# Attention on one core: VectorE's share of the exponentials without a mask pass, nine groups in place of eight, the last head's products in a score buffer

## The chip, the core and the metric

The kernel runs on one core of a Trainium2 chip. A core has a matrix engine (TensorE, "PE" in the profile; its weight loads are "PEld"), a vector engine (VectorE, "DVE"), an activation engine (ScalarE, "ACT"), a general engine (GpSimd, "POOL") and a queue engine (SyncE, "SP") that here only issues transfers. They share an on-chip memory (SBUF) with 128 partitions and an accumulator memory (PSUM) that TensorE writes. The metric is the device time of one execution in microseconds (us); lower is better.

## What is computed

Softmax attention for 8 x 8 heads, each with 512 queries, 512 keys and a width of 64, in float32:

```
scores = einsum('bhqd,bhkd->bhqk', q, k) / sqrt(64)
attn   = exp(scores - rowmax);  attn = attn / rowsum
out    = einsum('bhqk,bhkd->bhqd', attn, v)
```

That is 64 heads x 512 x 512 = 16.8 million exponentials. The kernel leaves the row maximum out (the ratio is the same without it), works with fp16 operands, and gets the row sum from a column of ones that stands beside the values.

## The kernel before, in words

**Tiling.** Two heads make a pair, 32 pairs in all. The scores of one head are computed transposed, in four blocks of 128 keys x 512 queries. Two blocks make a group: one PSUM tile `st` of 128 x 1024 float32, of which there are three. There are 129 groups (the last two hold one block each); the first three are written out by hand in `first_pair`.

**The road of a group.** GpSimd casts q and k of a pair to fp16 (`cast`, L335; the values in L329). TensorE transposes them (`transposes`, L388), VectorE copies the transposes to SBUF (`copy`, L402), TensorE makes the two score blocks (`scores`, L425), and the exponential turns `st` into fp16 weights `pt`. Of the groups, most go to ScalarE (one activation, L430). The eight listed in `ON_DVE` go to VectorE: `raise_` (L447) scales the scores out of PSUM into a fixed-point integer `z`, whose high half will be the bits of an fp16 number; the first `pass_` (L463) masks the fraction out of `z` into `m`; four more passes (L475) evaluate a polynomial in `m` and add it to `z`, and the result's high half, read as fp16, is the exponential. All six work on 128 x 1024 elements; the raise reads PSUM, the other five read and write SBUF.

**Products.** For each 128 queries of a head, four matmuls with the weights as the stationary operand add up 128 x 65 outputs (`values`, L514): a unit. Seven units share a PSUM bank tile `o`, of which there are two, shared with the transposes. VectorE takes a reciprocal and multiplies (`normalise`, L489 and L491), and SP writes the head out (L500). The last head is done block by block as its exponentials come (`last_values`, L529), into one of these two tiles; its 128 x 256 results go out through two queues (L549).

**Order.** All engines work through fixed lists. Class `Plan` makes the order: it steps through time with a cost for each kind of work (`SLOT`, `EXP`, `COPY`, `NORM`, `RAISE`, `PASSES`, `V_UNIT`), gives TensorE scores when one of the three `st` is free and otherwise transposes or products, and gives VectorE a pass of the exponential only where no copy, norm or raise would become late by it (`LATE_COPY`, `LATE_NORM`; a pass's cost is multiplied with `MARGIN`). Loads are issued by SP six pairs ahead (`feed`). GpSimd's casts are held back (`hold`, `release`) and given a wait on a VectorE instruction, so that they begin at a raise, copy or norm.

**Start.** ScalarE and SP load k and q of the first pair head by head. `make_identity` builds the identity on GpSimd. Four casts of the first head follow, one of them on GpSimd (k of two tiles, L579, then q of the second head, L581). TensorE runs eight matmuls without use (L562), transposes (L600, L595), and waits in order: the second transpose of k needs GpSimd's cast, and the first scores (L605) stand behind it.

Of the kernel before, what the change touches and what calls it, by code (L numbers as in the profile page):

```python
# [7 lines left out]

FP32 = mybir.dt.float32
FP16 = mybir.dt.float16  # L10
U32 = mybir.dt.uint32

EXP = mybir.ActivationFunctionType.Exp
# [3 lines left out]
class Plan:  # L17
# [18 lines left out]
    COPY, NORM, RAISE = (615, 700), (307, 390), (1145, 1225)  # L36
    COPY_1 = (400, 490)
    NORM_COLUMN, PASS_DONE = 67, 80
    PASSES = (650, 1230, 1230, 1230, 1230)
    FIRST_EXP = 5260  # L40
    STEP = 5
    FIRST_UNIT = 4
    ON_DVE = (6, 19, 30, 45, 62, 78, 90, 101)

    LATE_NORM, LATE_COPY, HURRY, SOON, BACKLOG = 1300, 1400, 900, 80, 1000
    MARGIN, SLACK = 1.05, 0

    def __init__(self, groups, pairs, first):
        self.groups, self.pairs = groups, pairs
        self.pe, self.act, self.dve = 7000, self.FIRST_EXP, 7000  # L50
        self.m, self.tiled = first, True
        self.read = []
        self.exps = {}
        for m in range(first):
            self.act += self.EXP + self.EXP_FIXED
            self.exps[m] = self.act + self.EXP_DONE
            self.read.append(self.exps[m])
        self.tq = {0: 5800}
        self.next_t = 1
        self.part_t = 0  # L60
        self.banks = [5100, 5800]
        self.todo = [(g, h) for g in range(pairs) for h in range(2)]
        self.head = None
        self.units = self.FIRST_UNIT
        self.member = {b: m for m, grp in enumerate(groups) for b in grp}
        self.ready = []
        self.passes = []
        self.steps = []
# [20 lines left out]
    def scores(self, t):  # L89
        m, grp = self.m, self.groups[self.m]  # L90
        slots = 2 if len(grp) == 2 and 0 < grp[0][0] and grp[0][2] == grp[1][2] else 1
        on_dve = self.for_dve(m)
        if m % 4 == 0 and grp[0][0] > 0 and len(grp) == 2:
            self.note(t, "feed", grp[0][0])
        self.note(t, "scores", m, on_dve)
        t += (0 if self.tiled else self.INTO) + self.SLOT * slots
        self.tiled = True
        if on_dve:
            self.ready.append((t + self.TO_DVE, "raise", (m,)))
            self.read.append(1e9)  # L100
        else:
            begin = max(self.act, t + self.TO_ACT)
            self.act = begin + self.EXP * len(grp) // 2 + self.EXP_FIXED
            self.exps[m] = self.act + self.EXP_DONE
            self.read.append(self.exps[m])
        self.m += 1
        self.pe = t
# [19 lines left out]
            self.part_t = 0  # L127

    def wants(self, g, h, part):

        chunks = (part,) if (g, h) == (self.pairs - 1, 1) else range(4)
        return max(self.exps.get(self.member[(g, c, h)], 1e9) for c in chunks)

    def edge(self):

        u, first = self.units, self.FIRST_UNIT
        return u % 7 == 0 or u in (first, first + 8 * self.pairs - 4)

    def values(self, t):
        if self.head is None:  # L140
            for g, h in self.todo[:14]:
                if t >= self.wants(g, h, 0) and t >= self.ready_v(g):
                    break
            else:
                return False
            if self.edge() and self.bank(t) is None:
                return False
            self.todo.remove((g, h))
            self.head = (g, h, 0)
# [10 lines left out]
        self.note(t, "values", g, h, part, self.units, self.bank_v)  # L160
        self.full(t, self.V_UNIT)
        self.units += 1
        if self.edge() and (g, h) != (self.pairs - 1, 1):
            what = (self.begun, self.units - self.begun, self.bank_v)
            self.ready.append((self.pe + self.TO_DVE, "norm", what))
        self.head = (g, h, part + 1) if part < 3 else None
# [54 lines left out]

    def run(self):
        t = 0
        while self.m < len(self.groups) or self.todo or self.head or self.ready or self.passes:
            if t >= self.pe:
                self.step_pe(t)
            if t >= self.dve:
# [8 lines left out]
def kernel(  # L236
# [45 lines left out]
    ring = cpool.tile([P, NU, D], FP32, name="ring")  # L282
    vps = [cpool.tile([P, 2, NI, D + 1], FP16, name=f"vp{n}") for n in range(NV)]
    ident = cpool.tile([P, P], FP16, name="ident")
    ones = nc.const_aps.tensor(1.0, [P, S], mybir.dt.bfloat16)

    raw = {}
# [119 lines left out]
    def scores(m, on_dve):  # L407
# [2 lines left out]
        st = ps_st.tile([P, 2, S], FP32, tag="st", name=f"st_{m}")  # L410
        if on_dve:
            bits = dpool.tile([P, 2, S], U32, tag="pd", name=f"pd_{m}")
            pt = bits.bitcast(FP16).rearrange("p x (s n) -> p x s n", n=2)[:, :, :, 1]
        else:
            pt = ppool.tile([P, 2, S], FP16, tag="pt", name=f"pt_{m}")
        for x, (g, c, h) in enumerate(grp):
# [4 lines left out]
            else:  # L421
                s = slice(64 * h, 64 * h + 64)
                kc = tqk[g][s, 1, c * P : (c + 1) * P]
                qc = tqk[g][s, 0, :]
            nc.tensor.matmul(st[:, x, :], kc, qc, start=True, stop=True)  # L425
            blocks[(g, c, h)] = pt[:, x, :]
        if on_dve:
            raised[m] = {"st": st, "bits": bits}
# [8 lines left out]

    QUARTIC = (0.013185735294320473 * 2.0**-78, 0.1618325836988675 * 2.0**-26, -0.6832878102805021, 0.5087543266551143 * 2.0**26)  # L440

    def raise_(m):
        release(2)
        r = raised[m]
        r["z"] = wpool.tile([P, 2, S], U32, tag="z", name=f"z_{m}")
        dve(
            nc.vector.tensor_scalar(  # L447
                out=r["z"][:, :, :],
                in0=r["st"][:, :, :],
                scalar1=scale * 1.4426950408889634 * 2.0**26,  # L450
                scalar2=15 * 2.0**26,
                op0=AluOp.mult,
                op1=AluOp.add,
            )
        )

    def pass_(m, s):
        r = raised[m]
        if s == 0:
            r["m"] = wpool.tile([P, 2, S], U32, tag="m", name=f"m_{m}")  # L460
            r["y"] = wpool.tile([P, 2, S], FP32, tag="y", name=f"y_{m}")
            dve(
                nc.vector.tensor_scalar(  # L463
                    out=r["m"][:, :, :],
                    in0=r["z"][:, :, :],
                    scalar1=0x03FFFFFF,
                    scalar2=0x04000000,
                    op0=AluOp.bitwise_and,
                    op1=AluOp.bitwise_or,
                )  # L470
            )
            return
        n = s - 1
        dve(
            nc.vector.scalar_tensor_tensor(  # L475
                out=r["bits"][:, :, :] if n == 3 else r["y"][:, :, :],
                in0=r["m"][:, :, :] if n == 0 else r["y"][:, :, :],
                scalar=QUARTIC[n],
                in1=r["z"][:, :, :] if n == 3 else r["m"][:, :, :],
                op0=AluOp.mult if n == 0 else AluOp.add,  # L480
                op1=AluOp.add if n == 3 else AluOp.mult,
            )
        )

# [18 lines left out]

    def values(g, h, y, u, bank):

        if (g, h) == (LAST, 1):
            return last_values(y, bank)
        if y == 0:
            needed(g, "v")
            heads.append((g, h, u))  # L510
# [8 lines left out]
                stop=(c == NI - 1),  # L519
            )  # L520

    def last_values(c, bank):


        if c == 0:
            last["o"] = ps_x.tile([P, 7, D + 1], FP32, tag=f"x{bank}", name="o_last")
        o = last["o"]
        for x in range(NI):
            nc.tensor.matmul(  # L529
# [123 lines left out]
    with tc.manual_schedule():  # L653
# [9 lines left out]
        for g in (1, 4, 5):  # L663
            load(g, "v")
        make_identity(nc, ident)
        for n in range(NV):
            nc.vector.memset(vps[n][:, :, :, D : D + 1], 1.0)
        first_pair()
        for g, names in ((1, "kq"), (0, "v"), (2, "kq")):
# [8 lines left out]
            "raise": raise_,  # L678
            "copy": lambda g, b: copy(g),
            "pass": pass_,  # L680
            "norm": lambda u, n, b: normalise(u, n),
        }
        for what, *args in Plan(groups, NP, 3).run():
# [31 lines left out]
```

## Time and profile before

| | |
|---|---|
| time, three runs | 121.89, 122.06, 122.09 us; median 122.06 |
| span of the profiled execution | 120.3 us; its time around the span is not listed, the median is 1.8 us more |
| ScalarE busy | 112.9 us (94% of the span) |
| VectorE busy | 105.1 us (87%) |
| TensorE busy, as modelled | 102.5 us (85%) |
| GpSimd busy | 64.5 us (54%) |
| HBM traffic | 25.17 MB read, 8.39 MB written; 279 GB/s over the span |
| granted TensorE clock | 0.998 of full speed over the span |

The profile is of one execution. A row for a group of instructions gives the engine, the operation, output and inputs, how many there were, their busy time and mean length, and the idle time of that engine just before them with what ended it. The length of a VectorE or ScalarE row includes its last stage, so the next row of the engine often begins a little before the row ends; how fast an engine goes through equal rows is read from the distance of their starts. TensorE's ends are modelled, and GpSimd's rows are rough.

### The profile page before, as it was taken

How to read it: one execution, taken by the hardware profiler on the slowest of the kernel's cores; microseconds unless marked ns; L12 is line 12 of the kernel's file. 1: busy time of each engine (PE TensorE's matmuls, PEld its weight loads, DVE VectorE, ACT ScalarE, POOL GpSimd, SP SyncE). 2: the span in 40 equal slices, each digit the busy share in tenths (PEclk: the TensorE clock that was granted, in tenths of full speed). 3: DMA queues.
4: the chain of work that ended last, by engine and by line, in shares of the span. 5: the costliest groups of instructions: out<-in, count | busy, mean ns of one | idle time of the engine just before them, and what ended most of it. 6: DMA issues, size and time to landing. Idle time of an engine off the chain costs nothing.

```text
span 120.3 us, 4002 instructions
## 1 busy us (share of the span) xinstructions
PE 102.5 (85%) x1557; PEld 64.7 (54%) x1557; DVE 105.1 (87%) x177; ACT 112.9 (94%) x125; POOL 64.5 (54%) x101
## 2 busy tenths in 40 slices
PE   7969478986999898988997999888899869999970
PEld 2536135644656564746664566644666536676650
DVE  1548999999999999999999999998999998996261
ACT  4699999999999999999999999999999999999970
POOL 2368867999649655359544557285546524340000
PEclk9999999999999999999999999999999999999999
DMA  3999999999999999899999898999999951232353
GB/s 102 293 346 379 381 380 385 383 377 332 312 361 355 339 352 346 277 303 306 284 299 296 228 376 256 300 362 349 325 304 357 301 187 44 90 120 95 106 166 96
DMA packets 35604, 33.83 MB, mean 281 GB/s; under 512 B 2688, under 2 KB 35584, under 8 KB 35584
## 3 DMA queue, kind: packets, MB, share of 16 engines
q1 hardware_dynamic: 35152, 33.24, 83.9%
q10 hardware_dynamic: 432, 0.33, 0.8%
q8 instruction: 12, 0.20, 0.7%
q14 instruction: 8, 0.07, 0.2%
HBM read 25.17 MB, written 8.39 MB: 279 GB/s over the span
## 4 chain that ended last, share of the span: by engine, by line
ACT 40%; PE 28%; DVE 22%; issue 8%; ACTq 0%
ACT pt L430 40%; PE st L425 10%; PE o L514 10%; DVE y L475 7%; DVE tqk L402 4%; DVE ring L491 3%; DVE z L447 3%; PE st_0a L562 3%; PE tp L388 2%; DVE m L463 2%; DVE pd L475 1%; DVE rc L489 1%; DVE tqk L395 1%; PE st L605 1%; DVE qt L642 0%
## 5 line engine op out<-in xcount | busy, mean ns | idle before, releaser
L430 ACT ACTIVATE pt<-st 128x1024 f16<-128x1024 f32 (+1 forms) x118 | 108.0, 1206 | 0.8 <-PE st L425 0.6
L425 PE MATMUL st<-tqk 64*128 64x512 f16 x248 | 45.0, 382 | 6.8 <-ACT pt L430 5.9
L514 PEld LDWEIGHTS <-pt 128*128 128x128 f16 x944 | 35.7, 98 | 14.1 <-issue 11.3
L514 PE MATMUL o<-vp,pt 128*128 128x65 f16 x944 | 41.8, 194 | 1.3 <-DVE tqk L395 0.6
L335 POOL CAST qkp<-k 128x512 f16<-128x512 f32 x31 | 21.2, 683 | 21.4 <-DMA out_dram<-ring 4.0
L335 POOL CAST qkp<-q 128x512 f16<-128x512 f32 x30 | 19.4, 645 | 13.9 <-DVE y L475 6.5
L329 POOL CAST vp<-v 128x512 f16<-128x512 f32 x32 | 24.3, 765 | 4.2 <-DVE y L475 2.3
L388 PE MATMUL tp<-ident,qkp 128*128 128x128 f16 x248 | 19.8, 220 | 4.9 <-DVE tqk L402 3.6
L491 DVE TENSOR_TENSOR ring<-o,rc 128x448 f32<-128x448 f32 (+2 forms) x37 | 22.6, 612 | 1.3
L425 PEld LDWEIGHTS <-tqk 64*128 64x128 f16 x248 | 12.1, 93 | 20.4 <-issue 14.3
L388 PEld LDWEIGHTS <-qkp 128*128 128x128 f16 x248 | 14.5, 97 | 13.1 <-issue 7.5
L475 DVE SCALAR_TENSOR_TENSOR y<-y,m 128x1024 f32<-128x1024 f32 x16 | 21.1, 1319 | 0.0
L402 DVE COPY tqk<-tp 128x1024 f16<-128x1024 f16 x30 | 20.4, 681 | 0.1
L489 DVE RECIPROCAL rc<-o 128x7 f32<-128x7 f32 (+2 forms) x37 | 7.2, 196 | 5.3 <-PE o L514 5.2
L475 DVE SCALAR_TENSOR_TENSOR y<-m 128x1024 f32<-128x1024 uint32 x8 | 10.8, 1348 | 0.1
L475 DVE SCALAR_TENSOR_TENSOR pd<-y,z 128x1024 uint32<-128x1024 f32 x8 | 10.4, 1299 | 0.0
L447 DVE TENSOR_SCALAR z<-st 128x1024 uint32<-128x1024 f32 x8 | 9.7, 1218 | 0.6 <-PE st L425 0.5
L514 PE MATMUL o<-vp,pd 128*128 128x65 f16 x64 | 9.3, 194 | 0.0
L463 DVE TENSOR_SCALAR m<-z 128x1024 uint32<-128x1024 uint32 x8 | 6.5, 807 | 0.1
L514 PEld LDWEIGHTS <-pd 128*128 128x128 f16 x64 | 6.3, 98 | 0.0
L562 PE MATMUL st_0a<-const-bfloat16-1.0 128*128 128x512 bf16 (+1 forms) x11 | 3.3, 456 | 0.8 <-PEq L699 0.8
L578 ACT ACT_TABLE_LOAD x1 | 1.3, 1283 | 1.7 <-PEq L699 1.7
(44 smaller groups left out, 18.6 us busy)
## 6 DMA issues: line engine op xcount, KB each, us to landing
out_dram<-ring SPq DMA_DIRECT2D x63, 128.0 KB, 4.1
k<-in_k_dram SPq DMA_DIRECT2D x31, 256.0 KB, 4.8
q<-in_q_dram SPq DMA_DIRECT2D x31, 256.0 KB, 4.9
v<-in_v_dram SPq DMA_DIRECT2D x27, 256.0 KB, 5.4
v<-in_v_dram SPq DMA_DIRECT2D x10, 128.0 KB, 4.3
k<-in_k_dram ACTq DMA_DIRECT2D x2, 128.0 KB, 2.9
q<-in_q_dram SPq DMA_DIRECT2D x2, 128.0 KB, 2.6
out_dram<-obl SPq DMA_DIRECT2D x1, 64.0 KB, 1.6
```

The source lines that it names most:

```text
L329: return nc.gpsimd.tensor_copy(out=vps[g % NV][:, :, :, 0:D], in_=raw[g]["v"][:, :, :, :])
L335: return eng.tensor_copy(out=qkp[g][:, "qk".index(name)].rearrange("p i (h d) -> p h i d", h=2), in_=raw[g][name][:, :, :, :],)
L388: nc.tensor.transpose(tps[g][:, n, i, :], qkp[g][:, n, i, :], ident)
L402: nc.vector.tensor_copy(out=tqk[g][:, :, :], in_=tps.pop(g).rearrange("p n i c -> p n (i c)"))
L425: nc.tensor.matmul(st[:, x, :], kc, qc, start=True, stop=True)
L430: nc.scalar.activation(out=pt[:, 0:size, :], in_=st[:, 0:size, :], func=EXP, scale=scale)
L447: nc.vector.tensor_scalar(out=r["z"][:, :, :], in0=r["st"][:, :, :], scalar1=scale * 1.4426950408889634 * 2.0**26, scalar2=15 * 2.0**26, o ...
L463: nc.vector.tensor_scalar(out=r["m"][:, :, :], in0=r["z"][:, :, :], scalar1=0x03FFFFFF, scalar2=0x04000000, op0=AluOp.bitwise_and, op1=Alu ...
L475: nc.vector.scalar_tensor_tensor(out=r["bits"][:, :, :] if n == 3 else r["y"][:, :, :], in0=r["m"][:, :, :] if n == 0 else r["y"][:, :, :] ...
L489: nc.vector.reciprocal(out=rc[:, 0:n], in_=o[:, x : x + n, D : D + 1])
L491: nc.vector.tensor_tensor(out=ring[:, u % NU : u % NU + n, :], in0=o[:, x : x + n, 0:D], in1=rc[:, 0:n].broadcast_to([P, n, D]), op=AluOp. ...
L514: nc.tensor.matmul(os[u // 7][:, u % 7, :], blocks[(g, c, h)][:, y * P : (y + 1) * P], vps[g % NV][:, h, c, :], start=(c == 0), stop=(c == ...
```

## The change

- **The lift.** Before the scores of a group of VectorE's, TensorE now writes a constant into `st` with one extra matmul for each block: `lift[0]` (128 x 128, ones in partitions 0, 32, 64 and 96, zero elsewhere) times `lift[1]` (128 x 512, two constants in these rows). The scores add to it. The two tiles are made at the start by ten GpSimd `memset`s, which stand behind `make_identity` and ahead of the first casts.
- **The raise** multiplies by one constant and takes a maximum. The lifted score lies between 2^17 and 2^18 as a float32, so that the low 16 bits of its mantissa are the fraction.
- **The passes.** The mask pass and its tile `m` are gone. The four polynomial passes read the low 16 bits of `z` in place (as uint16 with a step of two) where they read `m`; the result stands in the low half of `pd` and not the high one.
- **Nine groups** go to VectorE in place of eight: (6, 17, 34, 46, 61, 68, 84, 97, 111) for (6, 19, 30, 45, 62, 78, 90, 101). ScalarE has one full group less. The planner's costs are changed, so the order of all engines changes.
- **The last head's products** go into a score buffer (`st`), and the planner places them by themselves, not as units.

```
@@ -8,6 +8,7 @@
 
 FP32 = mybir.dt.float32
 FP16 = mybir.dt.float16
+U16 = mybir.dt.uint16
 U32 = mybir.dt.uint32
 
 EXP = mybir.ActivationFunctionType.Exp
@@ -36,14 +37,15 @@
     COPY, NORM, RAISE = (615, 700), (307, 390), (1145, 1225)
     COPY_1 = (400, 490)
     NORM_COLUMN, PASS_DONE = 67, 80
-    PASSES = (650, 1230, 1230, 1230, 1230)
+    PASSES = (1240, 1180, 1180, 1180)
+    OFFSET = 216
     FIRST_EXP = 5260
     STEP = 5
     FIRST_UNIT = 4
-    ON_DVE = (6, 19, 30, 45, 62, 78, 90, 101)
+    ON_DVE = (6, 17, 34, 46, 61, 68, 84, 97, 111)
 
     LATE_NORM, LATE_COPY, HURRY, SOON, BACKLOG = 1300, 1400, 900, 80, 1000
-    MARGIN, SLACK = 1.05, 0
+    MARGIN, SLACK = 1.0, 0
 
     def __init__(self, groups, pairs, first):
         self.groups, self.pairs = groups, pairs
@@ -60,6 +62,8 @@
         self.part_t = 0
         self.banks = [5100, 5800]
         self.todo = [(g, h) for g in range(pairs) for h in range(2)]
+        self.last = self.todo.pop()
+        self.last_part = 0
         self.head = None
         self.units = self.FIRST_UNIT
         self.member = {b: m for m, grp in enumerate(groups) for b in grp}
@@ -96,6 +100,7 @@
         t += (0 if self.tiled else self.INTO) + self.SLOT * slots
         self.tiled = True
         if on_dve:
+            t += self.OFFSET
             self.ready.append((t + self.TO_DVE, "raise", (m,)))
             self.read.append(1e9)
         else:
@@ -127,8 +132,7 @@
             self.part_t = 0
 
     def wants(self, g, h, part):
-
-        chunks = (part,) if (g, h) == (self.pairs - 1, 1) else range(4)
+        chunks = (part,) if (g, h) == self.last else range(4)
         return max(self.exps.get(self.member[(g, c, h)], 1e9) for c in chunks)
 
     def edge(self):
@@ -136,7 +140,20 @@
         u, first = self.units, self.FIRST_UNIT
         return u % 7 == 0 or u in (first, first + 8 * self.pairs - 4)
 
+    def last_values(self, t):
+        g, h = self.last
+        if self.m < len(self.groups) or self.last_part == 4 or t < self.read[-3]:
+            return False
+        if t < max(self.wants(g, h, self.last_part), self.ready_v(g)):
+            return False
+        self.note(t, "last", self.last_part)
+        self.full(t, self.V_UNIT)
+        self.last_part += 1
+        return True
+
     def values(self, t):
+        if self.last_values(t):
+            return True
         if self.head is None:
             for g, h in self.todo[:14]:
                 if t >= self.wants(g, h, 0) and t >= self.ready_v(g):
@@ -160,7 +177,7 @@
         self.note(t, "values", g, h, part, self.units, self.bank_v)
         self.full(t, self.V_UNIT)
         self.units += 1
-        if self.edge() and (g, h) != (self.pairs - 1, 1):
+        if self.edge():
             what = (self.begun, self.units - self.begun, self.bank_v)
             self.ready.append((self.pe + self.TO_DVE, "norm", what))
         self.head = (g, h, part + 1) if part < 3 else None
@@ -221,7 +238,7 @@
 
     def run(self):
         t = 0
-        while self.m < len(self.groups) or self.todo or self.head or self.ready or self.passes:
+        while self.m < len(self.groups) or self.todo or self.head or self.ready or self.passes or self.last_part < 4:
             if t >= self.pe:
                 self.step_pe(t)
             if t >= self.dve:
@@ -282,6 +299,7 @@
     ring = cpool.tile([P, NU, D], FP32, name="ring")
     vps = [cpool.tile([P, 2, NI, D + 1], FP16, name=f"vp{n}") for n in range(NV)]
     ident = cpool.tile([P, P], FP16, name="ident")
+    lift = [cpool.tile([P, n], FP16, name=f"lift{x}") for x, n in enumerate((P, S))]
     ones = nc.const_aps.tensor(1.0, [P, S], mybir.dt.bfloat16)
 
     raw = {}
@@ -410,7 +428,10 @@
         st = ps_st.tile([P, 2, S], FP32, tag="st", name=f"st_{m}")
         if on_dve:
             bits = dpool.tile([P, 2, S], U32, tag="pd", name=f"pd_{m}")
-            pt = bits.bitcast(FP16).rearrange("p x (s n) -> p x s n", n=2)[:, :, :, 1]
+            pt = bits.bitcast(FP16).rearrange("p x (s n) -> p x s n", n=2)[:, :, :, 0]
+            for x, (_, _, h) in enumerate(grp):
+                s = slice(64 * h, 64 * h + 64)
+                nc.tensor.matmul(st[:, x, :], lift[0][s], lift[1][s], start=True, stop=False)
         else:
             pt = ppool.tile([P, 2, S], FP16, tag="pt", name=f"pt_{m}")
         for x, (g, c, h) in enumerate(grp):
@@ -422,7 +443,7 @@
                 s = slice(64 * h, 64 * h + 64)
                 kc = tqk[g][s, 1, c * P : (c + 1) * P]
                 qc = tqk[g][s, 0, :]
-            nc.tensor.matmul(st[:, x, :], kc, qc, start=True, stop=True)
+            nc.tensor.matmul(st[:, x, :], kc, qc, start=not on_dve, stop=True)
             blocks[(g, c, h)] = pt[:, x, :]
         if on_dve:
             raised[m] = {"st": st, "bits": bits}
@@ -437,48 +458,41 @@
 
 
 
-    QUARTIC = (0.013185735294320473 * 2.0**-78, 0.1618325836988675 * 2.0**-26, -0.6832878102805021, 0.5087543266551143 * 2.0**26)
+    LIFT, STEP = (793.0, -0.039614853593207044), scale * 1.4426950408889634 * 1024
+    QUARTIC = tuple(
+        x * 65536.0**n
+        for n, x in enumerate((-22.8615461, 17.9701791, 3.89093568)[::-1], 1)
+    ) + (1.34267018e-02 * 1024 * 2.0**-64,)
 
     def raise_(m):
         release(2)
         r = raised[m]
-        r["z"] = wpool.tile([P, 2, S], U32, tag="z", name=f"z_{m}")
+        r["z"] = wpool.tile([P, 2, S], FP32, tag="z", name=f"z_{m}")
         dve(
             nc.vector.tensor_scalar(
                 out=r["z"][:, :, :],
                 in0=r["st"][:, :, :],
-                scalar1=scale * 1.4426950408889634 * 2.0**26,
-                scalar2=15 * 2.0**26,
+                scalar1=STEP,
+                scalar2=2.0**17,
                 op0=AluOp.mult,
-                op1=AluOp.add,
+                op1=AluOp.max,
             )
         )
 
     def pass_(m, s):
         r = raised[m]
+        f = r["z"].bitcast(U16).rearrange("p x (s n) -> p x s n", n=2)[:, :, :, 0]
         if s == 0:
-            r["m"] = wpool.tile([P, 2, S], U32, tag="m", name=f"m_{m}")
             r["y"] = wpool.tile([P, 2, S], FP32, tag="y", name=f"y_{m}")
-            dve(
-                nc.vector.tensor_scalar(
-                    out=r["m"][:, :, :],
-                    in0=r["z"][:, :, :],
-                    scalar1=0x03FFFFFF,
-                    scalar2=0x04000000,
-                    op0=AluOp.bitwise_and,
-                    op1=AluOp.bitwise_or,
-                )
-            )
-            return
-        n = s - 1
+        last = s == 3
         dve(
             nc.vector.scalar_tensor_tensor(
-                out=r["bits"][:, :, :] if n == 3 else r["y"][:, :, :],
-                in0=r["m"][:, :, :] if n == 0 else r["y"][:, :, :],
-                scalar=QUARTIC[n],
-                in1=r["z"][:, :, :] if n == 3 else r["m"][:, :, :],
-                op0=AluOp.mult if n == 0 else AluOp.add,
-                op1=AluOp.add if n == 3 else AluOp.mult,
+                out=r["bits"][:, :, :] if last else r["y"][:, :, :],
+                in0=r["y"][:, :, :] if s else f,
+                scalar=QUARTIC[s],
+                in1=r["z"][:, :, :] if last else f,
+                op0=AluOp.mult if last else AluOp.add,
+                op1=AluOp.add if last else AluOp.mult,
             )
         )
 
@@ -503,8 +517,6 @@
 
     def values(g, h, y, u, bank):
 
-        if (g, h) == (LAST, 1):
-            return last_values(y, bank)
         if y == 0:
             needed(g, "v")
             heads.append((g, h, u))
@@ -519,11 +531,11 @@
                 stop=(c == NI - 1),
             )
 
-    def last_values(c, bank):
-
-
+    def last_values(c):
         if c == 0:
-            last["o"] = ps_x.tile([P, 7, D + 1], FP32, tag=f"x{bank}", name="o_last")
+            needed(LAST, "v")
+            o = ps_st.tile([P, 2, S], FP32, tag="st", name="o_last")
+            last["o"] = o[:, 0, 0 : NI * (D + 1)].rearrange("p (x d) -> p x d", x=NI)
         o = last["o"]
         for x in range(NI):
             nc.tensor.matmul(
@@ -663,6 +675,10 @@
         for g in (1, 4, 5):
             load(g, "v")
         make_identity(nc, ident)
+        for t, xs in zip(lift, ((1.0, 1.0), LIFT)):
+            nc.gpsimd.memset(t[:, :], 0.0)
+            for p in range(4):
+                nc.gpsimd.memset(t[32 * p : 32 * p + 1, :], xs[p % 2])
         for n in range(NV):
             nc.vector.memset(vps[n][:, :, :, D : D + 1], 1.0)
         first_pair()
@@ -678,6 +694,7 @@
             "raise": raise_,
             "copy": lambda g, b: copy(g),
             "pass": pass_,
+            "last": last_values,
             "norm": lambda u, n, b: normalise(u, n),
         }
         for what, *args in Plan(groups, NP, 3).run():
```

## The prediction

> **What bounds the kernel now.** I read the page's head first, then ScalarE's instructions in order of time, then the groups, the waits, and at last the first microseconds.
>
> ```profile
> PE 102.5 (85%) x1557; PEld 64.7 (54%) x1557; DVE 105.1 (87%) x177; ACT 112.9 (94%) x125; POOL 64.5 (54%) x101
> ```
>
> ScalarE is the fullest. Its own timeline says where it is not:
>
> ```profile
> 4.88 0.60 ACT L612 ACTIVATE pt<-st_0a 128x512 f16<-128x512 f32 x1 [0.25 <-PE st_0a L605]
> ...
> 8.89 6.53 ACT L430 ACTIVATE pt<-st 128x1024 f16<-128x1024 f32 x7 [0.18 <-PE st L425]
> 15.69 16.15 ACT L430 ACTIVATE pt<-st 128x1024 f16<-128x1024 f32 x17 [0.27 <-PE st L425]
> 31.99 84.56 ACT L430 ACTIVATE pt<-st 128x1024 f16<-128x1024 f32 x93 [0.15 <-PE st L425]
> ```
>
> From the first exponential at 4.88 to the last at 116.55 it stops three times, 0.60 us together. From 31.99 it goes without a stop: 91 full groups and two half ones in 84.56 us, so 84.56 / 92 = 0.92 us a group. The end is fixed by three things: when ScalarE starts (4.88), how many groups it has, and what follows its last one (120.3 - 116.55 = 3.75 us: four products, a reciprocal, a multiplication, the last transfer). The other engines matter only where they make ScalarE wait.
>
> ```profile
> L463 DVE TENSOR_SCALAR m<-z 128x1024 uint32<-128x1024 uint32 x8 | 6.5, 807 | 0.1
> L447 DVE TENSOR_SCALAR z<-st 128x1024 uint32<-128x1024 f32 x8 | 9.7, 1218 | 0.6 <-PE st L425 0.5
> L475 DVE SCALAR_TENSOR_TENSOR y<-y,m 128x1024 f32<-128x1024 f32 x16 | 21.1, 1319 | 0.0
> L475 DVE SCALAR_TENSOR_TENSOR y<-m 128x1024 f32<-128x1024 uint32 x8 | 10.8, 1348 | 0.1
> L475 DVE SCALAR_TENSOR_TENSOR pd<-y,z 128x1024 uint32<-128x1024 f32 x8 | 10.4, 1299 | 0.0
> ```
>
> These rows price VectorE's exponential: (9.7 + 6.5 + 21.1 + 10.8 + 10.4) / 8 = 7.31 us a group. Taken one by one, a pass of L475 lasts between 1.215 and 1.636 us; the long ones lie where GpSimd is busy. The waits show what room the others have:
>
> ```profile
> PE st L425 <- ACT pt L430: 5.9, 16, 0.5
> DVE rc L489 <- PE o L514: 5.2, 6, 2.2
> ```
>
> TensorE waits 5.9 us for ScalarE to give a score buffer back. VectorE waits 5.2 us for products; its own timeline has nearly all of that behind 101 us, and between 9.5 us and there it hardly stops. So both have room, but VectorE's lies at the end.
>
> **The change part by part.**
>
> *ScalarE.* One full group fewer: 1 x 0.92 us off the engine that sets the end.
>
> *VectorE.* A new group is one raise (1.218; same shape, from PSUM) and four passes. Uint16 read with a step of two is in no row here. Nearest rows: two SBUF inputs of 1024 elements, uint32 or float32, all in L475. Bounds: 1.215 (the shortest) gives 9 x (1.218 + 4 x 1.215) = 54.7 us; 1.636 (the longest) gives 9 x (1.218 + 4 x 1.636) = 69.9 us. I take 1.31, between the means of the three rows, since the passes lie beside the same casts: 9 x 6.46 = 58.1 against 8 x 7.31 = 58.5 us. So nine groups cost VectorE what eight did, 0.4 us less, and that is off the path. Its cover is the 5.2 us of waits at its end. At 1.636 the surplus is 11.4 us, and 6 us of it would come through: a rival.
>
> *Copies between the passes.* ScalarE's stop of 0.27 us at 15.69 follows a copy that stood behind raise, mask and first pass on VectorE:
>
> ```profile
> 11.71 1.04 DVE L463 TENSOR_SCALAR m<-z 128x1024 uint32<-128x1024 uint32 x1
> 12.78 1.51 DVE L475 SCALAR_TENSOR_TENSOR y<-m 128x1024 f32<-128x1024 uint32 x1
> 14.21 0.68 DVE L402 COPY tqk<-tp 128x1024 f16<-128x1024 f16 x1
> ```
>
> In the new order this copy stands behind raise and first pass alone, some 1.0 us earlier. Bounds: all three stops gone (-0.60) or equal stops elsewhere (0 gained). I take half of the 0.27: -0.13. The second group goes in earlier (17 for 19), which leaves less than the whole.
>
> *TensorE.* Two lift matmuls a group, 18 in all. Two score matmuls span 0.39 us in the timeline and four 0.60, so a pair adds 0.21: 9 x 0.21 = 1.9 us; if the pair does not overlap, twice that, 3.8. Both lie under the 5.9 us. Queued behind a lift on TensorE are that group's scores, for VectorE's raise, and the next group's, for ScalarE, 0.2 us later; with three score buffers ScalarE has a group or two in hand. Taken at nothing; bound +0.3, if one such delay falls on each of two early stretches without a lead. The last head's products move from an `o` tile to an `st` tile that is free by then: in the old tail only the last four matmuls (0.31 us) stand behind ScalarE's last group, and still do. Before the last scores TensorE's new list has twelve more products (12 x 0.033 = 0.4 us, from the 32 that took 1.07 us of weight loads); its gaps there, 0.33 and 0.42 us, cover them. On SP the loads keep their order, and the 63 stores are bunched otherwise (up to four together); loads go out six pairs ahead. Nothing.
>
> *The memsets at the start.* GpSimd's rows there:
>
> ```profile
> 0.24 0.10 POOL L699 MEMSET const-float32-0.0<- 128x1 f32 x1 [0.24 <-issue]
> 0.27 0.10 POOL L699 MEMSET const-float32-1.0<- 128x1 f32 x1
> 0.31 0.10 POOL L699 MEMSET const-bfloat16-1.0<- 128x1 bf16 x1
> 0.34 0.10 POOL L699 MEMSET const-uint8-127<- 128x1 uint8 x1
> 0.73 0.20 POOL masks.py:197 MEMSET ident<- 128x128 f16 x1 [0.29 <-POOLq L699]
> 1.01 0.29 POOL masks.py:199 TENSOR_SCALAR_AFFINE_SELECT ident<-ident 128x128 f16<-128x128 f16 x1
> 3.53 0.29 POOL L579 CAST k<-k 128x128 f16<-128x128 f32 x1 [2.23 <-DMA k<-in_k_dram]
> ```
>
> A memset of one element takes 0.10, of 128 elements 0.20: 0.8 ns an element, so 0.53 for 512. The gap from 1.30 to 3.53 must hold all ten, with four waits on GpSimd's own work (0.08 each, from 0.93 to 1.01). One after another: 5 x 0.20 + 5 x 0.53 + 4 x 0.08 = 4.0 us, ready at 5.3, which is 1.75 late. Behind this cast stand the transpose of k at 4.02 (it could take the cast 0.15 later), in TensorE's order the first scores at 4.55, and so ScalarE: +1.6 us. If the memsets of one partition overlap as the four constants do (0.035 apart, each 0.10 long), the sum is 0.20 + 0.31 + 0.53 + 0.64 + 0.32 = 2.0 us, ready at 3.3, and the cast waits for its data as before: 0. I take 0, since four consecutive memsets without a wait are just what those rows show overlapped; both ends go into the range.
>
> On this the Trainium skill, GPSIMD Engine Reference, section Instruction dispatch, says that each of eight GpSimd cores serves its own 16 partitions and starts the next instruction as soon as its share is done. Rows 0, 32, 64 and 96 are four cores, so by the rule the sum is the one with 0; without overlap it is +1.6. No run here shows it yet.
>
> A rule of the skill speaks against the change: VectorE: DVE Perf Modes, on what auto-detection checks, lets two-input instructions go faster only for 16-bit data with a step of one. These have a step of two, so by it no pass is shorter for being 16 bits wide, and the mask pass (807 ns against 1319) was the cheapest to lose.
>
> *Sum.* -0.92 - 0.13 + 0 + 0 = -1.05 us on a span of 120.3. I put the same difference to the median, 1.8 us above that span: 122.06 - 1.05 = 121.0.
>
> **The rivals.**
>
> *The memsets come one after another.* The other side. For it: no row shows memsets of one partition or of 512 elements; against it: the constants' spacing. Price +1.0 (waits overlapped, only element time added: 4 x 0.11 + 4 x 0.43 us and the rest as above gives 4.8) to +1.6, so 122.06 - 1.05 + 1.0 to 1.6 = 122.0 to 122.6. It decides once the first cast starts later than 3.53 + 0.15 + 1.05 = 4.7 us.
>
> *ScalarE starves on the way.* Nine groups at new places, with a TensorE list that puts lifts ahead of scores, make some copy or score late. For it: VectorE has no stop of its own from 9.5 to 101 us, and the planner's pass (1180 to 1240, no margin) is below the 1299 to 1348 of the rows less the 80 ns or so by which starts overlap ends. Against it: the old plan was as far off early (1.5 us passes) and cost 0.6 us in stops. Price 0.5 to 1.4 us of new stops: 121.5 to 122.4.
>
> *VectorE's new passes are slow* (16-bit reads with a step): above 1.45 us a pass the nine groups cost 63 us and the 5 us at the end are gone; at 1.636 it is 122.06 - 1.05 + 6 = 127. For it: no row with such an operand; against it: uint32 and float32 inputs have one minimum, 1.215.
>
> *The change does nothing*: the end set by loads and not by ScalarE. Against it: the last loads are done by 96 us (the DMA slices fall there), and ScalarE never names a transfer after 4.3 us.
>
> **How the numbers follow.** My case 0.55 (120.6 to 121.4: all stops gone and a little more, or none gained and +0.3), memsets in turn 0.19, starving 0.18, slow passes 0.06, nothing 0.02. 0.2% is 0.24 us, about what these runs (121.89 to 122.09) can tell from no change: faster below 121.82, slower above 122.30. Faster: 0.55 and half of starving, 0.64. Slower: slow passes, half of the memsets, a part of starving, 0.22. Same: the rest, 0.14. The range from 120.6 to 122.5 leaves out the slow passes, the top of the memsets and a tail below. The likeliest case has 120.6 to 121.4 by itself.
>
> **What would show it.** ScalarE: 117 activations of L430 in place of 118, its first exponential still at 4.9, stops of at most 0.6 us, its last end near 115.5. GpSimd's first cast of k at 3.5; at 4.5 or later the memsets decide. Passes of VectorE with a mean of 1.25 to 1.35 and its waits for products still some 4 us at the end. The wait of TensorE for ScalarE's buffers down from 5.9 to 4. I am wrong if ScalarE starts late, if its stops between 5 and 115 us sum to over 1 us, or if a pass passes 1.45 us.

## The result, and the profile after

The changed kernel takes 124.15 us (median of four runs, 124.03 to 124.41) against 122.05 for the kernel before: a ratio of 1.0183, 95% interval 1.0167 to 1.0199. That is 2.1 us slower where 1.05 us faster was forecast, and outside the range. Medians, ranges and ratios in this document are of executions in the faster of the two states in which this chip runs a kernel; the few in the slower one, over 1.5% above that kernel's fastest, are left out. The profiled execution took 124.03 us with a span of 122.2; 1.8 us lie around it, as before.

The page's head for the changed kernel (busy time, share of the span, instructions):

```profile
PE 106.1 (87%) x1575; PEld 66.2 (54%) x1575; DVE 104.8 (86%) x174; ACT 111.9 (92%) x124; POOL 67.5 (55%) x111
```

ScalarE has 1.0 us less work, as intended, and is still the fullest. Its timeline (start, length, engine, line and operation, count, in brackets the idle time before and what ended it) shows where the time is:

```profile
6.90 0.60 ACT L624 ACTIVATE pt<-st_0a 128x512 f16<-128x512 f32 x1 [2.41 <-PE st_0a L617]
7.40 0.59 ACT L624 ACTIVATE pt<-st_0b 128x512 f16<-128x512 f32 x1
7.87 1.03 ACT L624 ACTIVATE pt<-st 128x1024 f16<-128x1024 f32 x1
9.41 1.02 ACT L624 ACTIVATE pt<-st 128x1024 f16<-128x1024 f32 x1 [0.51 <-PE st L617]
10.33 1.02 ACT L451 ACTIVATE pt<-st 128x1024 f16<-128x1024 f32 x1
11.79 11.10 ACT L451 ACTIVATE pt<-st 128x1024 f16<-128x1024 f32 x12 [0.45 <-PE st L446]
23.77 94.73 ACT L451 ACTIVATE pt<-st 128x1024 f16<-128x1024 f32 x104 [0.87 <-PE st L446]
```

The first exponential starts at 6.90 in place of 4.88: +2.02 us. Behind it ScalarE stops for 0.51 + 0.45 + 0.87 = 1.83 us, where it stopped for 0.60: +1.23. One group less gives -0.92. The last exponential ends at 118.50 (23.77 + 94.73) in place of 116.55, so +1.95; the 0.38 us between this and the sum of the three are, as far as the rows tell, small gaps of the old early stretch (17 exponentials in 16.15 us from 15.69, 0.95 each, against 0.92 later). The tail behind it is 3.7 us as before.

GpSimd's timeline says why the start is late:

```profile
1.25 0.21 POOL L679 MEMSET lift<- 128x128 f16 x1
1.52 0.90 POOL L681 MEMSET lift<- 1x128 f16 x4
2.48 0.53 POOL L679 MEMSET lift<- 128x512 f16 x1
3.07 2.24 POOL L681 MEMSET lift<- 1x512 f16 x4
...
5.37 0.29 POOL L591 CAST k<-k 128x128 f16<-128x128 f32 x1
```

The memsets of one partition do not overlap. Four of 512 elements take 2.24 us, 0.56 each, as much as one of 128 x 512 (0.53), and no row of the second to the fourth waits for a semaphore. The cast of k starts at 5.37; its data was there by 3.5, when the kernel before starts it.

The stop of 0.87 us has another cause. Of TensorE's waits (engine and line, what ended the wait, total, times, longest) two lines matter:

```profile
PE o L526 <- POOL vp L347: 1.3, 1, 1.3
PE st L446 <- ACT pt L451: 6.0, 13, 0.5
```

The first is new. It is one wait of 1.3 us at 22.99 us: a product that needs GpSimd's cast of the values of pair 1. Behind it in TensorE's list stand scores for ScalarE. In the old list the products of pair 1 stand behind the scores of group 20, in the new one directly behind those of group 17, since the faster exponential of group 6 (pair 1) is planned to be done earlier (at 18.7 us in place of 19.8 by the planner's own times); the planner takes the values of pair 1 as ready at 10.6 us (`ready_v`).

### The profile page after: what moved, and what is told of

It is laid out like the page before. It is cut to its first block, busy times and chain, and to the rows that moved or that the text cites. A ratio compares the mean times of both kernels' runs of the same rounds, so it can differ in the third digit from the quotient of the medians.

```text
span 122.2 us, 4038 instructions
## 1 busy us (share of the span) xinstructions
PE 106.1 (87%) x1575; PEld 66.2 (54%) x1575; DVE 104.8 (86%) x174; ACT 111.9 (92%) x124; POOL 67.5 (55%) x111
## 4 chain that ended last, share of the span: by engine, by line
PE 23%; DMA 21%; ACT 20%; DVE 20%; SPq 6%; issue 6%; POOL 2%; POOLq 0%; ACTq 0%
ACT pt L451 20%; DMA k<-in_k_dram 18%; PE o L526 9%; PE st L446 9%; DVE y L489 6%; DVE ring L505 5%; PE tp L406 4%; DMA q<-in_q_dram 4%; SPq L341 3%; DVE z L472 3%; DVE pd L489 2%; SPq L514 2%; DVE tqk L420 2%; DVE rc L503 2%; POOL qkp L353 1%
## 5 line engine op out<-in xcount | busy, mean ns | idle before, releaser
L451 ACT ACTIVATE pt<-st 128x1024 f16<-128x1024 f32 (+1 forms) x117 | 106.8, 1150 | 1.3 <-PE st L446 1.3
L353 POOL CAST qkp<-q 128x512 f16<-128x512 f32 x30 | 20.1, 668 | 14.7 <-DVE y L489 9.4
L489 DVE SCALAR_TENSOR_TENSOR y<-y,z 128x1024 f32<-128x1024 f32 x18 | 22.9, 1273 | 0.0
L489 DVE SCALAR_TENSOR_TENSOR pd<-y,z 128x1024 uint32<-128x1024 f32 x9 | 12.2, 1353 | 0.0
L489 DVE SCALAR_TENSOR_TENSOR y<-z 128x1024 f32<-128x1024 uint16 x9 | 11.7, 1299 | 0.1
L526 PE MATMUL o<-vp,pd 128*128 128x65 f16 x72 | 10.9, 195 | 0.5 <-DVE pd L489 0.3
L472 DVE TENSOR_SCALAR z<-st 128x1024 f32<-128x1024 f32 x9 | 10.9, 1213 | 0.0
L526 PEld LDWEIGHTS <-pd 128*128 128x128 f16 x72 | 7.0, 98 | 2.6 <-DVE pd L489 1.4
L434 PE MATMUL st<-lift,lift 64*128 64x512 f16 x18 | 3.5, 382 | 0.2 <-ACT pt L451 0.2
L574 PEld LDWEIGHTS <-const-bfloat16-1.0 128*128 128x128 bf16 x15 | 1.9, 143 | 2.4 <-issue 2.4
```

Of the source, the lines that this page charges most:

```text
L353: return eng.tensor_copy(out=qkp[g][:, "qk".index(name)].rearrange("p i (h d) -> p h i d", h=2), in_=raw[g][name][:, :, :, :],)
L451: nc.scalar.activation(out=pt[:, 0:size, :], in_=st[:, 0:size, :], func=EXP, scale=scale)
L472: nc.vector.tensor_scalar(out=r["z"][:, :, :], in0=r["st"][:, :, :], scalar1=STEP, scalar2=2.0**17, op0=AluOp.mult, op1=AluOp.max,)
L489: nc.vector.scalar_tensor_tensor(out=r["bits"][:, :, :] if last else r["y"][:, :, :], in0=r["y"][:, :, :] if s else f, scalar=QUARTIC[s], ...
L526: nc.tensor.matmul(os[u // 7][:, u % 7, :], blocks[(g, c, h)][:, y * P : (y + 1) * P], vps[g % NV][:, h, c, :], start=(c == 0), stop=(c == ...
L574: nc.tensor.matmul(dst[:, 0:n], ones[:, 0:P], ones[:, 0:n], start=True, stop=True)
```

## The experiments

Two causes are tested: the late start, and the order of work. Each run has the kernel before beside it on the same chip, and the ratio is to that. The experiments ran on three chips, so kernels are compared by their ratios first.

### The memsets taken away, and the memsets alone

`two_memsets` builds the same constant from two whole-tile memsets:

```
-        for t, xs in zip(lift, ((1.0, 1.0), LIFT)):
-            nc.gpsimd.memset(t[:, :], 0.0)
-            for p in range(4):
-                nc.gpsimd.memset(t[32 * p : 32 * p + 1, :], xs[p % 2])
+        for t, x in zip(lift, (1.078125, 11.4921875)):
+            nc.gpsimd.memset(t[:, :], x)
```

> The changed kernel with the lift built by two whole-tile memsets (1.078125 and 11.4921875; 64 products of them sum to the same constant) in place of ten. The start theory: GpSimd's first cast is back at 3.5 us, the first exponential at 4.9 in place of 6.90 (2.0 us), and if the three stops of ScalarE behind it (0.51, 0.45 and 0.87 us) were only the late start's, about 120.9 to 121.3 us. The rival, that the new order of work loses by itself: the start is back but the stop of 0.87 us near 23 us stays, about 122.

`before_ten` puts the four removed lines into the kernel before, behind `make_identity`:

> The kernel before with nothing new but the ten memsets behind the identity, on tiles that nobody reads. The start theory: the first cast near 5.4, the first exponential near 6.9, and the old kernel at 124 to 125 us. The rival, that the memsets cost less and the rest of the change costs the time: below 123.

Measured: `before_ten` 123.77 us (123.21 to 124.36), ratio 1.0126 (1.0061 to 1.0191); its profiled execution has the first exponential at 6.90, as in the changed kernel, and took 124.36. So the memsets by themselves cost the old kernel some 1.5 us (0.7 to 2.3 by the interval). `two_memsets` has most of its start back (first exponential at 5.19), and yet takes 123.96 us, ratio 1.0153 (1.0096 to 1.0210). ScalarE's timeline of `two_memsets`:

```profile
5.19 0.60 ACT L624 ACTIVATE pt<-st_0a 128x512 f16<-128x512 f32 x1 [0.54 <-PE st_0a L617]
...
9.38 11.17 ACT L451 ACTIVATE pt<-st 128x1024 f16<-128x1024 f32 x12 [0.20 <-PE st L446]
23.07 1.02 ACT L451 ACTIVATE pt<-st 128x1024 f16<-128x1024 f32 x1 [2.52 <-PE st L446]
24.39 1.94 ACT L451 ACTIVATE pt<-st 128x1024 f16<-128x1024 f32 x2 [0.29 <-PE st L446]
26.67 91.99 ACT L451 ACTIVATE pt<-st 128x1024 f16<-128x1024 f32 x101 [0.35 <-PE st L446]
```

The 1.7 us won at the start are lost again near 23 us, where the stop has grown from 0.87 to 2.52. The stop ends at about the same moment whenever the kernel starts: at 22.95 to 23.77 in the four kernels profiled with this order of work and these casts (the changed one, `two_memsets`, and `after_busy` and `no_lift` below), whose first exponentials lie between 4.84 and 6.90. That is the mark of something that comes at a fixed time, and the timeline of GpSimd and TensorE in `two_memsets` shows what:

```profile
18.27 0.61 POOL L353 CAST qkp<-k 128x512 f16<-128x512 f32 x1 [1.88 <-DMA k<-in_k_dram]
...
18.83 1.60 POOL L353 CAST qkp<-q 128x512 f16<-128x512 f32 x1
...
20.38 0.61 POOL L353 CAST qkp<-k 128x512 f16<-128x512 f32 x1
...
20.94 0.62 POOL L353 CAST qkp<-q 128x512 f16<-128x512 f32 x1
21.50 0.62 POOL L347 CAST vp<-v 128x512 f16<-128x512 f32 x1
22.17 0.22 PE L526 MATMUL o<-vp,pt 128*128 128x65 f16 x2 [2.26 <-POOL vp L347]
```

GpSimd works in order. The cast of the values of pair 1 (21.50) stands behind the casts of k and q of pairs 6 and 7, and the first of these waits for its load until 18.27. Between 5 and 30 us the DMA engines are busy nearly all the time, at a mean of 363 GB/s (371 in the kernel before).

The wait has a second price. TensorE is busy for only 1.15 us of the 3.41 us from 19.25 to 22.66, and from 22.66 to 26.08 the trace grants it half its clock (0.50): four score matmuls of 64 x 512 span 1.04 us at 23.74, where four in the changed kernel span 0.60 at 24.15. ScalarE's stops of 0.29 and 0.35 us lie there.

### The order of the casts, and of the products

`two_v1` moves one cast of `two_memsets`; the lists of the other engines stay:

```
-    FIRST_VALUES = {0: (), 1: (2,), 2: (3,), 3: (1,), 4: (5, 6), 5: (4, 7), 6: (8, 9)}
+    FIRST_VALUES = {0: (), 1: (2,), 2: (3, 1), 3: (), 4: (5, 6), 5: (4, 7), 6: (8, 9)}
```

> The run with two memsets, and GpSimd's cast of the values of pair 1 moved ahead of the casts of k and q of pairs 6 and 7 (it stood behind them, and the cast of k of pair 6 waits for its data to 18 us). Lists of TensorE, VectorE and ScalarE as in the changed kernel. If the 2.5 us stop of ScalarE near 23 us comes from TensorE's list, in which the products of pair 1 stand ahead of scores and wait 2.26 us for that cast, the stop goes and the time falls to 121.0 to 121.8. The rival, that the loads as a whole bound this stretch: the stop moves to the next pair's data and the time stays above 123.

`two_ready` leaves the casts of `two_memsets` and tells the planner the true time:

```
     def ready_v(self, g):
-        return 8300 + 2300 * g
+        return 21800 if g == 1 else 8300 + 2300 * g
```

> The run with two memsets, GpSimd's order left, and the planner told that the values of pair 1 are ready at 21.8 us and not at 10.6. TensorE's list then has their products behind the scores of group 23, not 17. If the place in TensorE's list is the cause, the 2.5 us stop goes here too, with no cast moved: 121.0 to 122.0. If the loads bound the stretch: above 123.

`after_v1` moves the cast in the changed kernel and leaves its ten memsets:

> The changed kernel, its ten memsets and late start left, with the cast of the values of pair 1 moved as in the other run. The two causes overlap: the late start (2.0 us at the first exponential) hides a part of the wait for that cast. With the wait alone gone, the stop of 0.87 us near 23 us goes and the start stays: 123.2 to 123.6. If the start were no cause at all: 121 to 122.

| run | memsets | wait for values of pair 1 | us, median (range) | ratio to before |
|---|---|---|---|---|
| changed kernel | ten | there | 124.15 (124.03 to 124.41) | 1.0183 (1.0167 to 1.0199) |
| `two_memsets` | two | there | 123.96 (123.19 to 124.95) | 1.0153 (1.0096 to 1.0210) |
| `after_v1` | ten | gone, cast earlier | 123.42 (122.54 to 124.17) | 1.0070 (1.0018 to 1.0122) |
| `two_v1` | two | gone, cast earlier | 121.95 (121.20 to 122.81) | 0.9975 (0.9947 to 1.0004) |
| `two_ready` | two | gone, products later | 121.60 (121.24 to 122.70) | 0.9968 (0.9937 to 0.9999) |

By the ratios, the memsets taken away alone give back 0.3% (within 0.6 of that, so perhaps nothing), the wait alone 1.1% (within 0.5), both together 2.1%. The times alone do not settle whether both give more than the sum, but the traces show that the causes hide each other: a kernel that starts 2 us late also asks for the values of pair 1 later, and the stop near 23 us grows from 0.87 to 2.52 when the start is moved forward. In the profiled executions of `after_v1` and `two_v1` a stop of 0.5 us stays near 22 us, where TensorE waits 0.2 to 0.3 us for a copy of VectorE's and no longer for the cast. The rival that the loads bound the whole stretch falls, since one cast moved within GpSimd's list is enough; in `two_v1` that cast runs right behind the one of pair 3, done at 17.0 us, and waits for no data. ScalarE's timeline of `two_ready`, whose profiled execution took 121.31 us (span 119.5):

```profile
4.98 0.60 ACT L624 ACTIVATE pt<-st_0a 128x512 f16<-128x512 f32 x1 [0.28 <-PE st_0a L617]
...
9.06 14.06 ACT L451 ACTIVATE pt<-st 128x1024 f16<-128x1024 f32 x15 [0.20 <-PE st L446]
23.31 34.26 ACT L451 ACTIVATE pt<-st 128x1024 f16<-128x1024 f32 x37 [0.19 <-PE st L446]
57.77 58.01 ACT L451 ACTIVATE pt<-st 128x1024 f16<-128x1024 f32 x64 [0.20 <-PE st L446]
```

Start and stops (0.59 us) are those of the kernel before, and the last exponential ends at 115.78, 0.77 us earlier than its 116.55. Against the kernel before, the two versions without both causes are 0.3% faster, 0.3 to 0.4 us, with intervals that reach to about no difference.

### The lift, the last head, the ninth group

`no_lift`, `nolift_v1` and `nolift_ready` take the lift out of `two_memsets`, `two_v1` and `two_ready` (they leave out the lower bound at 2^17):

```
-                nc.tensor.matmul(st[:, x, :], lift[0][s], lift[1][s], start=True, stop=False)
...
-                scalar2=2.0**17,
+                scalar2=STEP * (LIFT[0] + LIFT[1]),
                 op0=AluOp.mult,
-                op1=AluOp.max,
+                op1=AluOp.add,
```

> As the run with two memsets, in the same order of work, but without the lift: no memsets, no lift matmuls, and the raise adds the constant itself in place of the maximum (it leaves out the lower bound at 2^17, which this data does not reach). If 18 lift matmuls lie beside other work, as the prediction has it, the time is that of the run with two memsets within 0.2 us. If they hold up ScalarE's scores it is 0.3 to 1 us faster.

> The run without lift and memsets, with the cast of the values of pair 1 moved. Neither cause is left, nor the 18 lift matmuls: 121.0 by the prediction's sum, equal to the run with two memsets and the moved cast within 0.2 us. If the lifts cost: 0.3 to 1 us faster than that run.

> No lift and no memsets, the raise adds the constant (without the lower bound), and the planner knows the true time of pair 1's values. All known causes are gone: 121.0 to 121.3, no slower than the run with two memsets and that planner; if the lifts cost anything it shows here as a gain of over 0.2 us.

Measured: 123.87 us beside 123.96 (ratios 1.0135 and 1.0153); 121.75 beside 121.95 (0.9960 and 0.9975); 122.08 (121.27 to 122.47) beside 121.60 (0.9995 and 0.9968). Twice within 0.2 us, and once 0.5 slower, so no gain from taking the 18 lifts away shows: they lie beside other work. The third pair missed its expectation, and why is not shown. One thing that moves such runs is seen in the profiled execution of `nolift_ready`, the longest of its twelve (123.31 us) and not in its median: ScalarE stops for 1.74 us near 9 us, because the load of k of pair 1 is there only at 7.68 us, against 5.92 in the kernel before; GpSimd's row of `nolift_ready` for it:

```profile
7.68 0.61 POOL L352 CAST qkp<-k 128x512 f16<-128x512 f32 x1 [3.16 <-DMA k<-in_k_dram]
```

This load's time differs between executions (6.88 in one of the next kernel), and the twelve and ten runs of these two kernels spread by 2.0 and 1.4 us. A difference of 0.5 us between two medians is therefore not read as more than that.

`ready_lastx` puts the last head's products of `two_ready` back into an `o` tile, by the old lines of `last_values` and the planner:

> The run with two memsets and the true time of pair 1's values, with the last head's products back in an o tile as in the kernel before. The prediction costs this part at nothing: same as that run within 0.2 us (its profiled execution 121.3). The rival, that the score buffer frees the o tiles in the tail and hides the products there: 0.2 to 0.5 us slower.

Measured 121.57 us (120.93 to 122.35), ratio 0.9942 (0.9904 to 0.9980), beside 121.60 and 0.9968: no difference shows. The place of these products costs nothing and brings nothing that these runs can tell. This is the best ratio of all versions tried, 0.6% below the kernel before.

`ready_eight` gives group 61 of `two_ready` back to ScalarE:

```
-    ON_DVE = (6, 17, 34, 46, 61, 68, 84, 97, 111)
+    ON_DVE = (6, 17, 34, 46, 68, 84, 97, 111)
```

> The run with two memsets and the true time of pair 1's values, with eight groups on VectorE (61 goes back to ScalarE). By the sum, one group on ScalarE is 0.92 us: 0.8 to 1.0 us slower than that run, its last exponential at 116.6 to 116.8 in place of 115.78. The rival, that ScalarE is not what sets the end any more: the same time.

Measured 123.76 us (123.53 to 124.56), ratio 1.0140 (1.0070 to 1.0209), 2.2 us slower than `two_ready`; 0.8 to 1.0 was expected. The last exponential ends at 117.90 in place of 115.78, +2.12: one group more is 0.92, the start of this execution 0.16, and its list of work has six stops behind the start with 1.34 us where the other has three with 0.59, so +0.75. The last 0.3 us are not accounted for. So ScalarE does set the end, and the rival falls; but a list planned anew moved the time by as much again, and what the ninth group is worth by itself this run does not separate.

### The price of a memset, and the clock

`memset_prices` is the kernel before with twenty memsets:

> The kernel before with twenty memsets behind the identity, to read their rows: four of one partition and 512 elements on one tile at partitions 0, 32, 64, 96; four of one partition on four tiles, all at partition 0; four of 128 x 512; four of 128 x 1; four of 1 x 1 at partitions 0, 32, 64, 96. If memsets of one partition run in turn whatever the partition, the first two sets and the third take the same 0.53 us each, 6.4 us in all. If different partitions overlap, the first set takes under 1 us. The 128 x 1 and 1 x 1 sets tell whether short ones overlap, as the constants' rows 0.035 us apart suggest. The time itself is only the late start: about 129 us.

GpSimd's timeline of it, the five sets in that order:

```profile
1.25 2.18 POOL L672 MEMSET one<- 1x512 f16 x4
3.48 1.98 POOL L674 MEMSET four<- 1x512 f16 x4
5.42 1.99 POOL L676 MEMSET whole<- 128x512 f16 x4
7.36 0.19 POOL L678 MEMSET thin<- 128x1 f16 x4
7.50 0.49 POOL L680 MEMSET tiny<- 1x1 f16 x4
```

The element time is paid in turn in all three long sets: 0.5 us for 512 elements, for one partition as for 128, at four partitions of one tile as at one partition of four tiles. (Four partitions of four tiles were not run.) Only the fixed 0.1 us overlaps (`thin`: four in 0.19). On one tile at four partitions even single elements do not (0.49 for four); why is not shown. The first exponential came at 9.59 us and the one execution took 126.09 us, less than the 129 expected: some 2.2 us of the memsets fit into GpSimd's wait for its load, so the cast starts at 8.05, 4.5 us late.

`after_busy` fills TensorE's idle time at the start of the changed kernel:

```
         t_k(pka[:, 0], 0, 0)
+        for n in range(3):
+            busy(st0[:, 0], S)
         t_k(pkc[:, 0], 0, 1)
```

> The changed kernel with three more matmuls without use (128 x 512, about 0.43 us each on a cold clock) on TensorE between the two transposes of k, where it stands idle for 1.1 us waiting for GpSimd's late cast. If the idle time cost TensorE its fast clock, the rows after the cast shorten (two 64 x 512 scores from 0.64 to 0.39), the first exponential comes at about 6.6, the 0.51 and 0.45 us stops shrink, and the time falls by 0.5 to 1.2 us to 123.0 to 123.6. If the clock is not it: 124.1, same as the changed kernel.

Measured 123.21 us (123.19 to 124.09), ratio 1.0103 (1.0040 to 1.0165). Two score matmuls at the start of `after_busy` span 0.39 us:

```profile
6.56 0.39 PE L617 MATMUL st<-qt,kt 64*128 64x512 f16 x2
```

and in the changed kernel:

```profile
6.87 0.64 PE L617 MATMUL st<-qt,kt 64*128 64x512 f16 x2
```

The first exponential came at 6.47, and ScalarE's stops of 0.51 and 0.45 us shrank to 0.21 in all, while the stop near 23 us grew from 0.87 to 1.27. Between these two executions, TensorE's slow rows cost some 0.4 us at the first exponential and 0.7 us behind it, and hide 0.4 us of the other cause. But `after_v1`, without these matmuls, had 0.39 and 6.48 in its profiled execution too.

The trace says when the clock came. Its record of the granted clock begins with the step to full speed (the time before it is not in the record, and the mean that the profile lists counts it as 1.00): at 9.83 us in the changed kernel and 10.08 in `before_ten`, at 3.85 in the kernel before, 3.73 in `after_busy` and 4.46 in `after_v1`. TensorE's rows shorten at these times. In `after_busy` the step comes before the first filler matmul (4.39), so in that execution the filler did not bring it. The Trainium skill, TensorE: Matmul & The Clock Gate, section The HAM clock gate, says that the clock is released after a busy window of 3.4 us that runs freely. The trace agrees: from one step to the next it has 3.41 us or a whole multiple (6.83 in `no_lift`, 17.07 in `two_memsets`), and in the changed kernel TensorE was busy for 2.10 us of the 3.42 before 6.42, which hold the 1.1 us wait for the late cast, and for 3.33 of the 3.41 before the step at 9.83. In `two_v1`, whose cast is not late, the window from 3.09 to 6.50 was busy throughout and the step came at 6.50.

So a late cast fits as the cause of the late step, where the windows happen to fall across TensorE's wait; no run moves the windows on purpose. That the filler prevents it is not shown either, though three of its four runs lie within 0.02 us at 123.2.

## Why the prediction was wrong, point by point

- **"I take 0, since four consecutive memsets without a wait are just what those rows show overlapped".** This step failed. The constants' rows show the fixed 0.10 us overlapped and have no element time to speak of. The other end of the same bound was right: ten in turn "ready at 5.3", measured 5.31, and +1.6 at the first exponential, measured +1.60 in `after_v1` (6.48). The changed kernel's +2.02 has 0.42 more, since TensorE there had no full clock before 9.83; the prediction has no such term. The rival with chance 0.19 was the case.
- **The rule that went with it**, the Trainium skill, GPSIMD Engine Reference, section Instruction dispatch (each core serves its 16 partitions and goes on by itself): by it the four memsets of a set overlap. `memset_prices` measures 2.18 us for four, so for these memsets the measurement decides against it.
- **"Against it: the old plan was as far off early" (starving, 0.18).** This is the second step that failed. The price fits, 0.5 to 1.4 us against +1.23, but by luck: 0.96 of the 1.83 us of stops come from the late and slow start, and with the start moved forward (`two_memsets`) the stops sum to 3.36 us, +2.76. The mechanism was not named. What the prediction left out is what a faster exponential sets free: its products move up in TensorE's list, and there they wait for a cast behind a load. The profile of before showed the load side (GpSimd's waits for transfers); the step that compares both lists stopped at the tail ("twelve more products") and did not look at 15 to 25 us.
- **The rivals as one or the other.** Both came, and the range ended at 122.5. Their prices add up to 122.06 - 1.05 + 1.0 to 1.6 + 0.5 to 1.4, that is 122.5 to 124.0, against 124.15; that it comes so near is partly luck, since neither price holds by itself.
- **ScalarE, -0.92.** Right in its size: 117 activations, and 0.77 us off the last exponential once both causes are gone (`two_ready`). The -0.13 for the early copy did not come: the stop of 0.27 us is gone, but others stand elsewhere, 0.59 us in all against 0.60. The times with both causes gone lie between nothing and 0.6% below the kernel before in five versions (ratios 0.9942 to 0.9995), so by the ratios less than the forecast 1.05 us.
- **VectorE.** Right: passes of 1.30 us (46.8 us for 36; predicted 1.31), the shortest 1.205, so a uint16 input with a step of two is read as fast as float32. Its waits for products are 4.8 us. The Trainium skill, VectorE: DVE Perf Modes, section What auto-detection actually checks, lets two-input instructions go faster only where all data is 16 bits wide with a step of one; these rows agree, though none here has such data.
- **TensorE.** Right in the sum (taking the lifts away gains nothing: `no_lift`, `nolift_v1`), wrong in what was to show it: its wait for score buffers stayed, 6.0 us against 5.9, where 4 was expected.
- **The last head's products and the stores.** For the products right: no effect (`ready_lastx`). For the stores no run tells.

## What to carry to other kernels

A set-up instruction on an engine that looks idle at the start is priced by what stands behind it in that engine's list; on GpSimd the memsets here cost their elements per partition, in turn, however few partitions they write. A wait of TensorE may cost more than its length: here 3.41 us at half its clock came behind a wait of 2.26 us. When a step is made faster, look for what its result sets free on the next engine, and compare the two lists there with the time at which every other input of that step arrives. If two causes may hide each other, take both away before judging either: here neither alone brought the time back to the kernel before, and both together did.

## What the runs showed that was not expected

- A memset on GpSimd slows VectorE's casts beside it: the cast of 128 x 256 at the start lasts 0.53 us and that of 128 x 128 0.62 in the changed kernel, 0.29 and 0.35 in the kernel before. In `memset_prices` the cast of 128 x 128 lasts 2.49 us beside memsets of 512 elements.
- The load of k of pair 1 lands between 5.0 us (`two_memsets`) and 7.7 us (`nolift_ready`) in executions whose loads up to there are issued alike, and a landing at 6.9 to 7.7 us costs ScalarE a stop of 1.1 to 1.7 us.
